# Quartered output matmuls for a state-space branch, its gated unit moved ahead of both halves of the other branch's projection, and one fixed order for the side matmuls

## The chip, the cores and the metric

The kernel runs on one core of a Trainium2 chip (trn2). The metric is device time in microseconds (us), the median of 3 runs. The engines are named as in the profile: PE (TensorE, matmuls), PEld (its weight loads), DVE (VectorE), ACT (ScalarE), POOL (GpSimd), SP (SyncE, which here only issues DMAs).

## The reference

One decoder block on 256 tokens of width 1024, all in float32. The normed input is projected by one matrix into seven parts, two branches are computed from them, merged through gates, projected, normed and added to the input; an MLP of hidden width 4096 follows.

```python
u = rms_norm(h, g_pre_mix)
z_ssm, z_q, z_k, z_v, z_ga, z_gb = split(u @ w_in)       # 512, 512, 512, 512, 1024, 1024
# branch A: S5, 32 groups x 16 channels, 64 complex states a group
x  = scan over time of (ab * x + bu)                      # ab, bu from lam, dt, b and z_ssm
y  = Re(C x) + d_skip * z_ssm
v  = gelu(y)
y_a = v * sigmoid(v @ w_glu + b_glu)                      # GLU
# branch B: causal attention, 8 heads x 64
y_b = softmax(q k^T / 8, causal) v
merged = sigmoid(z_ga) * (y_a @ w_branch_a) + sigmoid(z_gb) * (y_b @ w_branch_b)
h = h + rms_norm(merged @ w_out)
h = h + rms_norm(square(relu(rms_norm(h) @ w_ff1)) @ w_ff2)
```

## The kernel before

**Weights and main matmuls.** Every weight matrix is cut into pieces of 128 x 1024 floats (512 KB). SP loads a piece into one of 3 raw buffers (L154), ACT rounds it into a high part `w_hi` and DVE subtracts for a low part `w_lo` (both by `split`, L169 and L170), in 5 buffers; a raw buffer is free again when its `w_lo` is made. PE then does three matmuls for each product (high x high, high x low, low x high; `three`, L193 to L195). `chunk` runs this for 512 output columns with 256 tokens moving: 24 matmuls a piece. These are called the main matmuls here. The list `order` fixes the sequence of pieces: `ssm, k, q, v, ga0, ga1, gb0, gb1` (4 pieces each, numbers 0 to 31), then `bb0, glu, bb1, ba0, ba1` (2 each: branch B's projection in two halves, GLU, branch A's projection in two halves), then `wo` and the MLP.

**Side blocks.** The S5 state space and the attention are computed by small float32 matmuls between the main ones, each block inside `with soon()`. For S5 these are `transposes`, `states(0)`, `local`, `outputs(0)`, `states(1)`, `outputs(1)`; for the attention `scores`, `transposes`, `values` for two groups of heads, called by `att.group(0)` and `att.group(1)`. A float32 matmul runs as two instructions. `outputs(hf)` (L975) multiplies, for each of 8 pairs of groups, three full 128 x 128 weights by 64 moving columns: `Tl` with the input `U` (L982), `CA` with the two parts of the state `X` (L987), 24 matmuls a half. Its result has time steps and channels together on the partitions, four of one by 32 of the other; ACT applies gelu to it into `y` (L989).

**The shuffle.** GLU needs `v` with channels on the partitions and the steps along the row. `shuffle` makes it from `y` by 32 DMAs on SP's queue (L389), 16 for each half, each 32 partitions of 2 runs of 64 floats. `v` is then split into `v_h` and `v_l` and multiplied by the GLU weights; the result goes through sigmoid on ACT, a product on DVE and a split into `ya_h`, `ya_l`, which branch A's projection reads.

**What sets the order.** The code gives each instruction a priority (`at`), and a scheduler places instructions of each engine by priority and by when it takes their inputs to be ready; `follow` ties one instruction behind another on its engine. Each engine then runs its own list strictly in that order. `soon()` gives each side block a priority of its own, ahead of the main matmuls, so that the matmuls of several side blocks that are ready at one time are mixed one by one. PSUM has 4 `acc` and 4 `aux` buffers; side blocks and branch A's projection share `aux` in turn.

Of the kernel before, what the change touches and what calls it, by code (L numbers as in the profile page):

```python
# [9 lines left out]
F32 = mybir.dt.float32  # L10
# [8 lines left out]
P = 128  # L19
# [27 lines left out]
PARAMS, MATS_B, ROTATE, MATS_C, LOCAL, STATES, OUT, SHUFFLE = 30, 31, 32, 33, 33, (34, 36), (35, 37), (35, 37)  # L47
# [28 lines left out]
def tile_hybrid_block(ctx, tc, a, out):  # L76
# [13 lines left out]

    def soon():

        state["soon"] += 1
        return at(SOON + 0.001 * state["soon"])
# [40 lines left out]
    order += [(n, range(2)) for n in ("bb0", "glu", "bb1", "ba0", "ba1")]  # L135
# [8 lines left out]
    state = {"i": 0, "soon": 0}  # L144
# [47 lines left out]
    def three(o, wh, wl, xh, xl, start, stop):  # L192
        nc.tensor.matmul(o, lhsT=wh, rhs=xh, start=start, stop=False)  # L193
        nc.tensor.matmul(o, lhsT=wh, rhs=xl, start=False, stop=False)  # L194
        return nc.tensor.matmul(o, lhsT=wl, rhs=xh, start=False, stop=stop)  # L195
# [7 lines left out]
    def chunk(kts, xh, xl, get=acc):  # L203

        ps = [get(), get()]
        marks.clear()
        for kp in range(kts // 2):
            hi, lo = piece()
            for k2 in range(2):
                for m in range(4):  # L210
                    kt = 2 * kp + k2
                    ws = slice(512 * k2 + P * m, 512 * k2 + P * m + P)
                    marks[kt] = three(ps[m // 2][:, m % 2, :], hi[:, ws], lo[:, ws], xh[:, kt, :], xl[:, kt, :],
                          start=(kt == 0 and m % 2 == 0), stop=(kt == kts - 1 and m % 2 == 1))
        return ps
# [192 lines left out]
    shuffle(1)  # L408
    with at(ATT[1]):
        att.group(1)  # L410
# [45 lines left out]
    gate(1, 0)  # L456
    branch_b(0)
# [12 lines left out]
    gate(1, 1)  # L470
    branch_b(1)
# [200 lines left out]
class S5:  # L672


    def __init__(self, nc, sp, scratch, aux, ident, aidx, half_pi, dsk, spare, table, soon):
# [4 lines left out]
        self.bc = sp.tile([P, 4, NI, 16], F32, name="bc", tag="bcy")  # L680
# [220 lines left out]
    def transposes(self):  # L901

        nc, B4 = self.nc, self.B4
        self.y = self.sp.tile([P, NI, NB], F32, name="y", tag="bcy")
        self.B4T = B4T = [t.rearrange("p i b c -> p i (b c)") for t in B4]
        for i4 in range(4):
            for j in range(2):
                tp = self.aux((P, 4, P))
                with self.soon():
                    for i in range(4):  # L910
                        nc.tensor.transpose(tp[:, i, :], B4T[j][:, 4 * i4 + i, :], self.ident)
                nc.scalar.activation(B4T[j][:, 4 * i4:4 * i4 + 4, :], tp, AF.Copy)

    def local(self):
# [3 lines left out]
        with self.soon():  # L918
# [222 lines left out]
```

## Time and profile before

| | |
|---|---|
| median of 3 runs | 390.36 us (389.51 to 392.51) |
| the profiled execution | 389.2 us, of it the span 387.4 us |
| PE busy | 372.2 us, 96% of the span |
| DVE, ACT, POOL busy | 69%, 55%, 9% |
| chain that ended last | PE 88%, DMA 4%, DVE 2%, ACT 2%, issue 2% |

The busy time of PE says how much of the span had a matmul under way, not how fast they ran. Idle time of another engine costs nothing unless PE waits for it. So the rows to read are those where PE was idle or its matmuls were further apart than usual, and what came just before on the engine that released it.

### The profile page before, as it was taken

The numbers are of one execution on the slowest core, as the hardware profiler recorded it, in microseconds if no ns is written. First come the engines' busy times: TensorE is split into PE (matmuls) and PEld (weight loads), VectorE is DVE, ScalarE is ACT, GpSimd is POOL, SyncE is SP. The second block draws the span as 40 slices with busy tenths as digits, with TensorE's granted clock in tenths as the row PEclk, the third lists the DMA queues.
The fourth block names the chain that finished last, engine by engine and source line by source line (L and its number), as shares of the span: only waits on it lengthen the run. The fifth ranks groups of instructions, "written<-read, shape, count | busy, mean of one in ns | idle before, by whom it ended". The sixth has DMA issues, their size and how long they took to land.

```text
span 387.4 us, 6661 instructions
## 1 busy us (share of the span) xinstructions
PE 372.2 (96%) x2593; PEld 337.0 (87%) x2593; DVE 268.5 (69%) x459; ACT 213.3 (55%) x322; POOL 36.7 (9%) x46
## 2 busy tenths in 40 slices
PE   7999999999999996889999999999999999999993
PEld 6999989999897986788877989989898998989882
DVE  5899999988886264579595575665638375664734
ACT  4894559968773872645457563534444444443411
POOL 4006200001000000000010020100202020020200
PEclk9999999999999998999999999999999999999998
DMA  7956755544305056555643665665555555556302
GB/s 209 359 171 205 231 185 168 161 151 154 112 15 175 12 157 221 168 165 187 216 156 106 215 207 192 207 203 194 184 181 191 200 190 184 194 183 191 137 1 108
DMA packets 22160, 66.30 MB, mean 171 GB/s; under 512 B 5200, under 2 KB 5840, under 8 KB 22000
## 3 DMA queue, kind: packets, MB, share of 16 engines
q1 hardware_dynamic: 21184, 65.19, 51.9%
q0 software_dynamic: 512, 0.53, 0.6%
q8 instruction: 20, 0.33, 0.3%
q10 hardware_dynamic: 432, 0.17, 0.2%
q14 instruction: 12, 0.10, 0.1%
HBM read 63.77 MB, written 1.05 MB: 167 GB/s over the span
## 4 chain that ended last, share of the span: by engine, by line
PE 88%; DMA 4%; DVE 2%; ACT 2%; issue 2%; SPq 0%; DVEq 0%; POOLq 0%; POOL 0%; ACTq 0%
PE acc L200 11%; PE acc L198 11%; PE acc L199 11%; PE aux L194 8%; PE aux L195 8%; PE aux L193 8%; PE acc L193 7%; PE acc L195 7%; PE acc L194 7%; DMA w_raw<-in_w_in_dram 3%; PE aux L987 2%; PE aux L950 2%; PE aux L1013 1%; DMA v<-y 1%; PE aux L982 1%
## 5 line engine op out<-in xcount | busy, mean ns | idle before, releaser
L170 DVE TENSOR_TENSOR w_lo<-w_raw,w_hi 128x1024 fp32r<-128x1024 f32 (+2 forms) x119 | 139.6, 1178 | 79.3 <-ACT w_hi L169 78.7
L169 ACT ACTIVATE w_hi<-w_raw 128x1024 fp32r<-128x1024 f32 (+2 forms) x119 | 121.2, 1024 | 127.1 <-PE aux L194 38.2
L193 PE MATMUL acc<-xh,w_hi 128*128 128x256 f32 x224 | 63.4, 287 | 0.9 <-ACT w_hi L169 0.9
L194 PE MATMUL acc<-xl,w_hi 128*128 128x256 f32 x224 | 63.1, 286 | 0.0
L193 PE MATMUL aux<-h_h,w_hi 128*128 128x256 f32 x224 | 62.9, 281 | 0.0
L194 PE MATMUL aux<-h_l,w_hi 128*128 128x256 f32 x224 | 62.6, 280 | 0.0
L195 PE MATMUL aux<-h_h,w_lo 128*128 128x256 f32 x224 | 62.5, 280 | 0.0
L195 PE MATMUL acc<-xh,w_lo 128*128 128x256 f32 x224 | 60.2, 286 | 0.0
L198 PE MATMUL acc<-w_hi,f_h 128*128 128x512 f32 x128 | 50.2, 394 | 0.0
L199 PE MATMUL acc<-w_lo,f_h 128*128 128x512 f32 x128 | 50.1, 393 | 0.0
L200 PE MATMUL acc<-w_hi,f_l 128*128 128x512 f32 x128 | 49.6, 391 | 0.0
L193 PEld LDWEIGHTS acc<-xh,w_hi 128*128 128x128 f32 x224 | 43.0, 192 | 1.9 <-ACT w_hi L169 1.8
L194 PEld LDWEIGHTS acc<-xl,w_hi 128*128 128x128 f32 x224 | 43.1, 192 | 0.2 <-issue 0.2
L194 PEld LDWEIGHTS aux<-h_l,w_hi 128*128 128x128 f32 x224 | 42.1, 188 | 0.3
L193 PEld LDWEIGHTS aux<-h_h,w_hi 128*128 128x128 f32 x224 | 42.0, 188 | 0.3
L195 PEld LDWEIGHTS aux<-h_h,w_lo 128*128 128x128 f32 x224 | 42.0, 188 | 0.0
L195 PEld LDWEIGHTS acc<-xh,w_lo 128*128 128x128 f32 x224 | 41.2, 191 | 0.8 <-issue 0.4
L68 POOL TENSOR_TENSOR r<-r 128x512 f32<-128x512 f32 x14 | 17.8, 1288 | 131.6 <-ACT f_h L634 131.6
L200 PEld LDWEIGHTS acc<-w_hi,f_l 128*128 128x128 f32 x128 | 24.1, 188 | 5.5
L198 PEld LDWEIGHTS acc<-w_hi,f_h 128*128 128x128 f32 x128 | 24.1, 188 | 5.1
L199 PEld LDWEIGHTS acc<-w_lo,f_h 128*128 128x128 f32 x128 | 24.1, 188 | 4.8
L636 DVE TENSOR_TENSOR f_l<-r,f_h 128x512 fp32r<-128x512 f32 x14 | 15.3, 1097 | 6.5 <-POOL r L68 6.5
(245 smaller groups left out, 582.1 us busy)
## 6 DMA issues: line engine op xcount, KB each, us to landing
w_raw<-in_w_ff_dram SPq DMA_DIRECT2D x64, 512.0 KB, 4.8
w_raw<-in_w_in_dram SPq DMA_DIRECT2D x31, 512.0 KB, 4.1
w_raw<-in_w_out_dram SPq DMA_DIRECT2D x8, 512.0 KB, 4.6
w_raw<-in_w_bb_dram SPq DMA_DIRECT2D x4, 512.0 KB, 4.5
w_raw<-in_w_ba_dram SPq DMA_DIRECT2D x4, 512.0 KB, 5.6
w_raw<-in_w_glu_dram SPq DMA_DIRECT2D x2, 512.0 KB, 4.5
x_tok<-in_xt_dram SPq DMA_DIRECT2D x1, 1024.0 KB, 4.8
g_row<-in_rows_dram SPq DMA_DIRECT2D x2, 512.0 KB, 4.5
```

Of the source, the lines that this page charges most:

```text
L68: return nc.gpsimd.tensor_tensor(o, x, y, op=op)
L169: i = nc.scalar.activation(hi, src, AF.Copy)
L170: j = nc.vector.tensor_tensor(lo, src, hi.bitcast(F32), op=ALU.subtract)
L193: nc.tensor.matmul(o, lhsT=wh, rhs=xh, start=start, stop=False)
L194: nc.tensor.matmul(o, lhsT=wh, rhs=xl, start=False, stop=False)
L195: return nc.tensor.matmul(o, lhsT=wl, rhs=xh, start=False, stop=stop)
L198: first = nc.tensor.matmul(o, lhsT=xh, rhs=wh, start=start, stop=False)
L199: nc.tensor.matmul(o, lhsT=xh, rhs=wl, start=False, stop=False)
L200: nc.tensor.matmul(o, lhsT=xl, rhs=wh, start=False, stop=stop)
L636: nc.vector.tensor_sub(f_l[:, js, :], r, f_h[:, js, :].bitcast(F32))
L950: nc.tensor.matmul(S[j][:, i, :], lhsT=self.B4T[j][:, hf * H + i, :], rhs=U4[:, hf * H + i, :], start=(i == 0), stop=(i == H - 1))
L987: nc.tensor.matmul(py[:, i, :], lhsT=CA[j][:, ii, 1:5, :].rearrange("p d c -> p (d c)"), rhs=self.X[j][:, i, :], start=False, stop=(i == H ...
```

## The change

Four edits. (1) `outputs` is made in quarters: for each block of 2 rows of channels, each of the 4 steps and each of the 3 sources, four matmuls of 32 weight columns write the four 32-partition quarters of one PSUM tile, so that the result already has the layout of `v`; gelu writes `v` itself. That is 96 matmuls a half, in place of 24. (2) `shuffle`, its 32 DMAs and the tile `y` are gone. (3) GLU comes in front of both halves of branch B's projection, in the list of pieces and in the program. (4) Side blocks have one common priority and are tied to each other: within a block each matmul comes where it did, and a block's first matmul follows the last of the block before it; the first matmul of each `chunk` follows the last of the chunk before. The attention's `group` is cut into `weights` (scores, softmax's exponentials) and `outputs` (normalise, transpose, values), called around the S5 blocks.

```diff
     def soon():
-        state["soon"] += 1
-        return at(SOON + 0.001 * state["soon"])
+        first = []
+        def side(inst):
+            if not first and "side" in last_act:
+                follow(inst, last_act["side"])
+            first[:] = [inst]
+        with at(SOON):
+            yield side
+        last_act["side"] = first[0]
...
-    order += [(n, range(2)) for n in ("bb0", "glu", "bb1", "ba0", "ba1")]
+    order += [(n, range(2)) for n in ("glu", "bb0", "bb1", "ba0", "ba1")]
...
-    def shuffle(hf):
-        with at(SHUFFLE[hf]):
-            for b in range(4):
-                for q in range(4):
-                    nc.sync.dma_start(out=v[32 * q:32 * q + 32, 2 * hf:2 * hf + 2, b, :],
-                                      in_=s5.y[32 * b:32 * b + 32, 8 * hf + q:8 * hf + 8:4, :])
...
     with at(LOCAL):
         s5.local()
+    att.bind(qT, kT, v_tok)
+    with at(ATT[0]):
+        att.weights(0)
     with at(OUT[0]):
-        s5.outputs(0, att)
+        s5.outputs(0, v)
     with at(STATES[1]):
         s5.states(1)
-    att.bind(qT, kT, v_tok)
     with at(ATT[0]):
-        att.group(0)
+        att.outputs(0)
+    with at(ATT[1]):
+        att.weights(1)
     with at(OUT[1]):
-        s5.outputs(1, att)
-    shuffle(0)
-    shuffle(1)
+        s5.outputs(1, v)
     with at(ATT[1]):
-        att.group(1)
+        att.outputs(1)
...
-    gate(1, 0)
-    branch_b(0)
     ps = chunk(4, v_h, v_l)
...
-    gate(1, 1)
-    branch_b(1)
+    for c in range(2):
+        gate(1, c)
+        branch_b(c)
...
-    def outputs(self, hf, att):
+    def outputs(self, hf, v):
-        py = self.aux((P, H, NB))
-        with self.soon():
-            for i in range(H):
-                ii = hf * H + i
-                nc.tensor.matmul(py[:, i, :], lhsT=self.Tl[:, ii].rearrange("p b c -> p (b c)"), rhs=U4[:, ii, :],
-                                 start=(i == 0), stop=False)
-            for i in range(H):
-                ii = hf * H + i
-                for j in range(2):
-                    nc.tensor.matmul(py[:, i, :], lhsT=CA[j][:, ii, 1:5, :].rearrange("p d c -> p (d c)"),
-                                     rhs=self.X[j][:, i, :], start=False, stop=(i == H - 1 and j == 1))
-        self.table("gelu", nc.scalar.activation(self.y[:, hf * H:hf * H + H, :], py, AF.Gelu_apprx_tanh), "sin", "exp")
+        py = self.aux((P, 2, L, NB))
+        with self.soon() as side:
+            for m, b, src in ((m, b, src) for m in range(2) for b in range(L) for src in range(3)):
+                for q in range(4):
+                    i = 4 * m + q
+                    ii = hf * H + i
+                    w = self.Tl[:, ii, b, :] if src == 2 else CA[src][:, ii, 1 + b, :]
+                    side(nc.tensor.matmul(py[32 * q:32 * q + 32, m, b, :], lhsT=w,
+                                          rhs=U4[:, ii, :] if src == 2 else self.X[src][:, i, :],
+                                          start=(m == b == src == 0), stop=(m == 1 and b == L - 1 and src == 2)))
+        self.table("gelu", nc.scalar.activation(v[:, 2 * hf:2 * hf + 2], py, AF.Gelu_apprx_tanh), "sin", "exp")
```

Where instructions move, at three places. Rows are in the engine's order; a row gives line, operation and out<-in, with a count where the same row repeats.

PE, the second half of S5 and the attention. Before, rows from `values(0)` (L1062), `outputs(1)` (L982) and `scores(1)` (L1013) stand mixed:

```order
L1062 MATMUL aux<-pT_365,v_tok 64x256 x2
L982 MATMUL aux<-U_122,Tl 128x64
L1013 MATMUL aux<-kT,qT 128x128
L982 MATMUL aux<-U_122,Tl 128x64
L1013 MATMUL aux<-kT,qT 128x128
L1062 MATMUL aux<-pT_366,v_tok 64x128 x2
L1013 MATMUL aux<-kT,qT 128x128
L982 MATMUL aux<-U_122,Tl 128x64
```

After the change the same stretch has `scores(1)` (L1019), then the new `outputs(1)` (L992) by itself:

```order
L1019 MATMUL aux<-kT,qT 128x256 x2
L992 MATMUL aux<-Er,CA_126 32x64 x4
L992 MATMUL aux<-Ei,CA_127 32x64 x4
L992 MATMUL aux<-U_122,Tl 32x64 x4
L992 MATMUL aux<-Er,CA_126 32x64 x4
L992 MATMUL aux<-Ei,CA_127 32x64 x4
```

The mixing of blocks is gone, and each matmul of `outputs` fills 32 of the 128 output partitions. PE alternates between main matmuls and side blocks 7 times before, from `outputs(0)` on, and 10 times after, from `scores(0)` on.

SP, the DMA issues from the last `w_in` pieces on. Before:

```order
L154 DMA w_raw<-in_w_glu_dram 128x1024
L389 DMA v<-y 32x2x64
L154 DMA w_raw<-in_w_bb_dram 128x1024
L389 DMA v<-y 32x2x64 x10
L154 DMA w_raw<-in_w_bb_dram 128x1024
L389 DMA v<-y 32x2x64 x3
L154 DMA w_raw<-in_w_ba_dram 128x1024
L389 DMA v<-y 32x2x64 x3
```

After:

```order
L163 DMA w_raw<-in_w_in_dram 128x1024 x28
L163 DMA w_raw<-in_w_glu_dram 128x1024 x2
L163 DMA w_raw<-in_w_bb_dram 128x1024 x4
L451 DMA x_tok<-in_xt_dram 128x2048
L452 DMA g_row<-in_rows_dram 128x1024
L163 DMA w_raw<-in_w_ba_dram 128x1024 x4
```

The shuffle's DMAs no longer stand between the weight loads; `x_tok` and `g_row` (1.5 MB) now stand ahead of all four `ba` loads, before they stood ahead of the last two.

ACT, behind the second gelu. Before, `y` is made just ahead of these rows (L989); sigmoids (L423) and the attention's copies (L1046, L1051, L1065) follow, and `v_h` comes last:

```order
L423 ACT_TABLE_LOAD
L423 ACTIVATE sg_106<-sg_106 128x512 x2
L423 ACTIVATE sg_105<-sg_105 128x512 x4
L169 ACTIVATE w_hi<-w_raw 128x1024
L1046 ACTIVATE pT_365<-aux 128x512 x2
L1051 ACTIVATE pT_366<-aux 128x512
L169 ACTIVATE w_hi<-w_raw 128x1024 x2
L423 ACTIVATE sg_106<-sg_106 128x512
L1065 ACTIVATE yb_h<-aux 128x512
L423 ACTIVATE sg_106<-sg_106 128x512
L169 ACTIVATE w_hi<-w_raw 128x1024
L169 ACTIVATE v_h<-v 128x512 x2
```

After (exponentials L1033, gelu L995, sigmoids L431, copies L1052, L1057):

```order
L1033 ACTIVATE prob_364,sm_370<-prob_364,mx_368 128x256 x2
L178 ACTIVATE v_h<-v 128x512
L995 ACT_TABLE_LOAD
L995 ACTIVATE v<-aux 128x512
L431 ACT_TABLE_LOAD
L431 ACTIVATE sg_106<-sg_106 128x512 x2
L431 ACTIVATE sg_105<-sg_105 128x512 x4
L1052 ACTIVATE pT_365<-aux 128x512 x2
L178 ACTIVATE v_h<-v 128x512
```

The first half of `v_h` moved ahead of the second gelu, the second half now stands behind six sigmoids and the copies of `pT`.

## Rows read from the trace of the kernel before

**Rows 1.** The page: the chain that ended last, shares of the span by engine and by line.

```profile
PE 88%; DMA 4%; DVE 2%; ACT 2%; issue 2%; SPq 0%; DVEq 0%; POOLq 0%; POOL 0%; ACTq 0%
```

**Rows 2.** Windows view, the stretch behind the longest wait: its length, busy time of each engine (PE, PEld, DVE, ACT, POOL) with the count of instructions, PE's granted clock as a share of full speed, share of the DMA engines, GB/s.

```profile
149.25:163.20 13.95, 12.79 (x97) 12.60 (x97) 6.71 (x8) 6.57 (x11) 0.00 (x0) 0.88 0.66 228
```

**Rows 3.** The chain that ended last in order of time, 140 to 177 us: start, length, what.

```profile
143.28 4.88 DMA v<-y
...
152.91 0.21 PE acc L194
...
153.50 0.12 PE acc L194
```

**Rows 4.** Timeline of PE at its waits, and GLU's last matmul: start, length, instruction, and in brackets the idle time before and what ended it.

```profile
149.25 0.50 PE L193 MATMUL acc<-v_h,w_hi 128*128 128x256 f32 x2 [3.30 <-ACT v_h L169]
...
159.47 0.28 PE L195 MATMUL acc<-v_h,w_lo 128*128 128x256 f32 x1
...
163.17 0.74 PE L193 MATMUL aux<-ya_h,w_hi 128*128 128x256 f32 x4 [1.15 <-ACT ya_h L169]
165.67 0.39 PE L194 MATMUL aux<-ya_l,w_hi 128*128 128x256 f32 x1 [1.76 <-DVE ya_l L170]
```

**Rows 5.** Timeline of PE, 174 to 180 us: the first `w_out` matmul, behind the last of branch A's projection.

```profile
176.22 0.39 PE L198 MATMUL acc<-w_hi,mg_h 128*128 128x512 f32 x1
```

**Rows 6.** SP's queue: ten of the shuffle's issues (start, length), and the DMA view's line for them (KB each, median us from issue to landing).

```profile
122.01 14.76 SPq L389 DMA_DIRECT2D v<-y  x10
```

```profile
v<-y SPq DMA_DIRECT2D x32, 16.0 KB, 2.3
```

**Rows 7.** Timeline of PE, full-width side matmuls in a block: 16 instructions of `outputs(0)` up to the next instructions, which are the last two of `states(1)`, and the 32 of `states(0)`.

```profile
101.67 2.00 PE L987 MATMUL aux<-X,CA 128*128 128x64 f32 x16
103.50 0.39 PE L950 MATMUL aux<-U,B 128*128 128x64 f32 x2
```

```profile
77.94 3.68 PE L950 MATMUL aux<-U,B 128*128 128x64 f32 x32
```

**Rows 8.** Windows of 40 ns inside one block of `local` (L925: 16 instructions of 32 weight columns, 128 moving columns, four output quarters in turn): window, length, PE (instructions under way), PEld (loads under way).

```profile
86.10:86.14 0.04, 0.02 (x3) 0.02 (x4) 1.00 0.00 0
86.14:86.18 0.04, 0.04 (x4) 0.04 (x8) 1.00 0.00 0
...
86.46:86.50 0.04, 0.04 (x12) 0.04 (x4) 1.00 0.00 0
```

**Rows 9.** The same in windows of 20 ns for L929 (8 instructions of 32 weight columns on 32 partitions, 32 moving columns, four quarters in turn).

```profile
86.70:86.72 0.02, 0.02 (x4) 0.02 (x4) 1.00 0.00 0
...
86.74:86.76 0.02, 0.02 (x6) 0.02 (x8) 1.00 0.00 0
```

**Rows 10.** Line view of L925: duration in ns (min/median/max) of a weight load of 32 columns.

```profile
L925 PEld LDWEIGHTS aux<-CA,B x64: 105/109/111, 82.3 to 87.9; 128*32 128x32 f32 x64
```

**Rows 11.** Timeline of PE: the first and the last of the mixed stretch (16 instructions of L1062, 12 of L982 and 8 of L1013 start in it), and the same kinds in blocks.

```profile
117.65 0.65 PE L1062 MATMUL aux<-pT,v_tok 128*64 128x256 f32 x4
...
124.33 0.66 PE L982 MATMUL aux<-U,Tl 128*128 128x64 f32 x4
```

```profile
96.91 0.71 PE L1013 MATMUL aux<-kT,qT 64*128 64x128 f32 x4
97.55 0.43 PE L982 MATMUL aux<-U,Tl 128*128 128x64 f32 x2
```

```profile
137.70 0.65 PE L1062 MATMUL aux<-pT,v_tok 128*64 128x256 f32 x4
138.28 0.39 PE L195 MATMUL acc<-xh,w_lo 128*128 128x256 f32 x1
...
139.17 1.09 PE L1062 MATMUL aux<-pT,v_tok 128*64 128x128 f32 x12
140.19 0.38 PE L195 MATMUL acc<-yb_h,w_lo 128*128 128x256 f32 x1
```

**Rows 12.** Timeline of PE: 50 main matmuls start between the first and the last of these.

```profile
88.42 0.39 PE L193 MATMUL acc<-xh,w_hi 128*128 128x256 f32 x1
88.65 0.28 PE L194 MATMUL acc<-xl,w_hi 128*128 128x256 f32 x1
...
94.42 0.33 PE L982 MATMUL aux<-U,Tl 128*128 128x64 f32 x2
```

**Rows 13.** Timeline of ACT: the second gelu, a table load, six sigmoids, two copies of `pT`.

```profile
130.44 0.60 ACT L989 ACTIVATE y<-aux 128x512 f32<-128x512 f32 x1
131.06 1.28 ACT L423 ACT_TABLE_LOAD   x1
132.35 3.24 ACT L423 ACTIVATE sg<-sg 128x512 f32<-128x512 f32 x6
...
136.45 1.06 ACT L1046 ACTIVATE pT<-aux 128x512 f32<-128x512 f32 x2
```

**Rows 14.** Timeline of DVE: a normalisation of the softmax, a `w_lo`, the last state of `states(1)`, and one of the masked maxima of `scores`.

```profile
113.25 1.13 DVE L1034 TENSOR_SCALAR prob<-prob,sm 128x256 f32<-128x256 f32 x4
114.30 1.22 DVE L170 TENSOR_TENSOR w_lo<-w_raw,w_hi 128x1024 fp32r<-128x1024 f32 x1
...
116.03 0.68 DVE L699 TENSOR_TENSOR Ei<-wpzA,wpzB 128x504 f32<-128x504 f32 x1
...
126.53 0.42 DVE L1020 CUSTOM_DVE_ANT_0 prob<-aux,shp 128x256 f32<-128x256 f32 x1 [0.77 <-PE aux L1013]
```

More of the change, by code (lines that the diff above doesn't have):

```diff
@@ L192, in three @@
     def three(o, wh, wl, xh, xl, start, stop):
[L193 removed]
+        first = nc.tensor.matmul(o, lhsT=wh, rhs=xh, start=start, stop=False)
         nc.tensor.matmul(o, lhsT=wh, rhs=xl, start=False, stop=False)
[L195 removed]
+        return first, nc.tensor.matmul(o, lhsT=wl, rhs=xh, start=False, stop=stop)
     def three_tok(o, xh, xl, wh, wl, start, stop):
@@ L212, in chunk @@
                     ws = slice(512 * k2 + P * m, 512 * k2 + P * m + P)
-                    marks[kt] = three(ps[m // 2][:, m % 2, :], hi[:, ws], lo[:, ws], xh[:, kt, :], xl[:, kt, :],
+                    first, marks[kt] = three(ps[m // 2][:, m % 2, :], hi[:, ws], lo[:, ws], xh[:, kt, :], xl[:, kt, :],
                           start=(kt == 0 and m % 2 == 0), stop=(kt == kts - 1 and m % 2 == 1))
+                    if earlier is not None:
+                        follow(first, earlier)
+                        earlier = None
         return ps
@@ L917, in local @@
         pt = self.aux((P, 4, P))
-        with self.soon():
+        with self.soon() as side:
             for ct in range(4):
@@ L946, in states @@
         S = [aux((P, H, NB)), aux((P, H, NB))]
-        with self.soon():
+        with self.soon() as side:
             for j in range(2):
                 for i in range(H):
-                    nc.tensor.matmul(S[j][:, i, :], lhsT=self.B4T[j][:, hf * H + i, :], rhs=U4[:, hf * H + i, :],
-                                     start=(i == 0), stop=(i == H - 1))
+                    side(nc.tensor.matmul(S[j][:, i, :], lhsT=self.B4T[j][:, hf * H + i, :], rhs=U4[:, hf * H + i, :],
+                                          start=(i == 0), stop=(i == H - 1)))
         er, ei, R = self.E[hf]
@@ L1008, in scores @@
         sc = [self.aux((P, 2, n)), self.aux((P, 2, n))]
-        with self.soon():
+        with self.soon() as side:
             for e in range(2):
@@ L1012, in scores @@
                     rows = slice(64 * par, 64 * par + 64)
-                    nc.tensor.matmul(sc[par][:, e, :], lhsT=self.qT[rows, 2 * g + e, qt * P:qt * P + P],
-                                     rhs=self.kT[rows, 2 * g + e, 0:n], start=(e == 0), stop=(e == 1))
+                    side(nc.tensor.matmul(sc[par][:, e, :], lhsT=self.qT[rows, 2 * g + e, qt * P:qt * P + P],
+                                          rhs=self.kT[rows, 2 * g + e, 0:n], start=(e == 0), stop=(e == 1)))
         return sc
@@ L1055, in values @@
         yp = self.aux((P, 2, T))
-        with self.soon():
+        with self.soon() as side:
             for e in range(2):
@@ L1061, in values @@
                         hc = slice(64 * (4 * g + h), 64 * (4 * g + h) + 64)
-                        nc.tensor.matmul(yp[64 * par:64 * par + 64, e, qs], lhsT=v_tok[:, kt, hc], rhs=pT[:, h, :],
-                                         start=(e == 0 and kt == 0), stop=(e == 1 and kt == 1))
+                        side(nc.tensor.matmul(yp[64 * par:64 * par + 64, e, qs], lhsT=v_tok[:, kt, hc], rhs=pT[:, h, :],
+                                              start=(e == 0 and kt == 0), stop=(e == 1 and kt == 1)))
         gs = slice(2 * g, 2 * g + 2)
@@ L1074, in group, with outputs @@
             self.exp(qt)
+    def outputs(self, g):
         for qt in range(2):
```

35 lines of the change are left out of this document (18 added, 17 removed).

## The prediction

> **What bounds the kernel now.** I read the shares of the chain that ended last first: PE holds 88% of it, DMA 4% [rows 1]. So the kernel is a PE kernel, and time is won where PE has less to do or waits less. The same chain in order of time shows the one long piece that is not PE: the shuffle's last DMA from 143.28 us, 4.88 us long [rows 3]. PE's timeline then gives the waits themselves. Before GLU's first matmul PE stood idle for 3.30 us, released by `v_h`. Before branch A's projection it stood idle for 1.15 and 1.76 us, released by `ya_h` and `ya_l` [rows 4]: GLU's last matmuls are just ahead there, and its sigmoid, product and split are exposed. [...] The chain's matmuls stand 0.21 us apart up to 152.91 us, and 0.12 from 153.50 on [rows 3]. Everything before the first side blocks and behind the first `w_out` matmul at 176.22 us [rows 5] runs the same instructions before and after.
>
> **Removed: the shuffle (3.3 + 1.7 us).** gelu writes `v`, so the 32 DMAs go, and with them the wait for the last of them. A shuffle DMA took 2.3 us from issue to landing, and ten of them held SP's queue for 14.76 us, weight loads behind them [rows 6]. All 3.30 us of idle time and the 1.7 us of slow clock go if no other wait of that length takes their place; that is the third rival.
>
> **Moved: GLU in front (2.9 us).** GLU's chain of sigmoid, product and split now has 96 matmuls of branch B's projection behind it, some 11 us of PE by 0.118 us a matmul (49 in 94.42 - 88.65 us [rows 12]). Before, the chain ran from GLU's last matmul at 159.47 us to the last release at 165.67, 6.2 us [rows 4]. That fits under 11, so 1.15 + 1.76 = 2.9 us go. The loads of `x_tok` and `g_row` are now ahead of all `ba` loads on SP; they are 1.5 MB, about 6.6 us at the 228 GB/s of [rows 2], and the first `ba` piece is needed 17 us of matmuls (GLU and both `bb` halves) after the last main chunk. This costs nothing.
>
> **Made anew: `outputs` (3.8 us won, from 0 to 5.8).** Before, 16 full-width instructions took 1.83 us, 0.114 each [rows 7], so the 48 of a half 5.5 us. After, a half has 96 matmuls, 192 instructions, in 48 groups of four quarters. Two rows bound a group. `local` does the same with 128 moving columns: the four instructions start together, and the four groups of a block start between 86.12 and 86.47 us, 0.115 us a group [rows 8]. L929 does it with 32 moving columns: one group starts by 86.70, the next by 86.755, 0.055 us [rows 9]. Here 64 columns move, and the straight line between gives 0.055 + 0.060 x 32 / 96 = 0.075 us, 3.6 us a half. I take that; the ends are 2.6 and 5.5 us. Two halves win 2 x (5.5 - 3.6) = 3.8 us.
>
> [...]
>
> **Untied: mixed side blocks (2.1 us).** From 117.65 to 124.33 us, 6.68 us, 16 instructions of L1062, 12 of L982 and 8 of L1013 ran mixed one by one. In blocks, 16 of L1062 took 0.58 + 1.02 = 1.60 us, and four of L1013 0.64 [rows 11]; 12 of L982 at 0.114 are 1.37. Together 4.25 us, so mixing cost 2.4 us. The new order has no mixing, but alternates with main matmuls three times more; the first main matmul behind a block took 0.23 us instead of 0.118 [rows 12], so 0.3 us is given back.
>
> **Added: waits of PE behind tied blocks (2.7 us lost).** All side blocks now wait for the one before, and PE runs its list in order, so a late block holds the main matmuls behind it, too. I walked PE's new list from 88.42 us, where `local` ends. `scores(0)` 2.4 us, 74 main matmuls 8.7, `outputs(0)` 3.6, `states(1)` 3.7 (as the 32 instructions of `states(0)` [rows 7]): 106.8 us. Then 12 transposes at 0.114, 72 main matmuls, `values(0)` 1.6, `scores(1)` 2.4 and `outputs(1)` 3.6 bring PE to the second group's transposes at about 124.2 us. They need the softmax normalised on DVE. Before, the last state of `states(1)` was made by 116.71 us, 13.0 us behind its last matmul at about 103.7 [rows 7, 14]. With the same chain it is made at 119.8 us now. Behind it stand `yb_l` (0.7, as the last state's 504 columns), eight maxima (four at 0.42 and four of half the width, 2.4), two `w_lo` (1.2 each) and two normalisations (1.13 and about 0.8 at half the width) [rows 14], 7.4 us: 127.2 us. Transposes of the first head can begin a little earlier, so PE loses about 2 us. At GLU I find no wait longer than 0.4 us: gelu, its table, sigmoids' table, six sigmoids and two copies are 7.5 us of ACT [rows 13] in front of `values(1)`, and PE has 48 main matmuls, 5.6 us, behind those transposes to cover them; `v_h` and gelu's table can run while DVE normalises. The first group's transposes find gelu(0) some 0.3 us late. Together 2.7 us.
>
> **The sum.** 3.3 + 1.7 + 2.9 + 3.8 + 2.1 - 2.7 = 11.1 us. The profiled execution took 389.2 us; the median of the runs is 390.36, 1.2 above it. So 378.1 us against that execution, and 379.3 as a median.
>
> **Rivals.** First: ACT and DVE set the pace from `states(1)` to GLU. For it speaks that DVE's chain is 13.0 us long and that the walk already ends in a wait for it; against it, all long waits of PE before lay behind this stretch [rows 4]. Then a faster `outputs` and the unmixing win nothing, the added waits are their own size: 3.3 + 1.7 + 2.9 = 7.9 us, 382.5 us.
>
> Second: weight loads of a quarter don't run beside the matmuls of other quarters. Then a group costs a load of 0.109 us [rows 10] and half of 0.115 for the matmul, 0.166 us, 8.0 a half. PE gets later by 8.8 us, which covers the 2.7 us of added waits: 11.1 - 8.8 + 2.7 = 5.0, 385.4 us. Against it, eight loads were under way beside four matmuls from 86.14 to 86.18 us [rows 8]. [...]
>
> Third: the wait moves instead of going. `v_h`'s second half now stands behind gelu, six sigmoids and the copies of `pT`; if that chain is 3 us late, PE idles in front of GLU as before and the clock falls again: 11.1 - 5.0 = 6.1, 384.3 us.
>
> Fourth, the other side: the quarters run one after another at a full-width instruction's 0.114 us. Then a half takes 192 x 0.114 = 21.9 us, 32.8 more for two. The other terms win 10.0 us, and PE is too late for the added waits: 390.36 + 32.8 - 10.0 = 413 us. It decides from 5.5 + 5.0 = 10.5 us a half on, 0.22 us a group, twice what [rows 8] show.
>
> **How the numbers follow.** The forecast gets 0.56, the first rival 0.22, the third 0.08, the second 0.06, the fourth 0.04; 0.04 is left for a group at its lower bound with no added wait, 374.6 us. The forecast's own range is 377 to 381.5. I predict 379.3 us, and 376.5 to 384.5 holds the forecast, the first rival and part of the third. One per cent of 390.36, about what a measurement of this kernel can tell from no change, ends at 386.5 and 394.3: faster 0.92, within it 0.04 (part of the second), slower 0.04.
>
> **What would show it.** `outputs`' 192 instructions in 3.6 us, 2.6 to 5.5; PE's idle time in front of GLU under 0.5 us and granted clock 1.0 from 130 to 165 us; no idle time in front of branch A's projection; the first `w_out` matmul near 165 us instead of 176.22; a wait of PE for DVE of some 2 us at the second transposes. I am wrong if a group of four takes more than 0.115 us, if PE idles in front of `values(1)` or GLU, or if gaps appear behind 176 us, where I assumed nothing changes.

## The result, and the profile after

The changed kernel takes 379.65 us (median of 4, 379.20 to 380.60), the kernel before 389.94 beside it: ratio 0.9728, 95% interval 0.9678 to 0.9778. In a second group of runs the same kernel took 378.68 us against 390.44 (ratio 0.9681, 0.9634 to 0.9727). The forecast was 379.3. The profiled execution has a span of 378.2 us, 9.2 less than before. Medians are of all runs, while the ratios leave out the few runs that the chip ran at a lower granted clock and some per cent longer.

The chain that ended last, shares by engine (before: [rows 1]):

```profile
PE 89%; DMA 3%; ACT 3%; issue 2%; DVE 1%; DVEq 0%; POOLq 0%; POOL 0%; ACTq 0%
```

The shuffle's piece of DMA is gone from the chain, ACT has one point more. PE's timeline where it had waited in [rows 4], and the first `w_out` matmul ([rows 5]): no brackets, so no idle time, in front of GLU or of branch A's projection.

```profile
138.01 0.28 PE L202 MATMUL acc<-v_h,w_hi 128*128 128x256 f32 x1
...
156.41 0.28 PE L202 MATMUL aux<-ya_h,w_hi 128*128 128x256 f32 x1
...
167.29 0.39 PE L207 MATMUL acc<-w_hi,mg_h 128*128 128x512 f32 x1
```

`outputs(1)` in the timeline: rows of 8 instructions stand 0.11 us apart, so four quarters take 0.056 us, and 24 such rows reach from 127.11 us to the first transposes at 129.93, where PE then waits for the normalised softmax.

```profile
127.11 0.32 PE L992 MATMUL aux<-Er,CA 128*32 128x64 f32 x8
127.25 0.29 PE L992 MATMUL aux<-Ei,CA 128*32 128x64 f32 x8
127.36 0.29 PE L992 MATMUL aux<-U,Tl 128*32 128x64 f32 x8
...
129.93 0.33 PE L1050 MATMUL aux<-shp,prob 128*128 128x128 f32 x1
130.97 0.33 PE L1051 MATMUL aux<-shp,prob 128*128 128x128 f32 x1 [0.71 <-DVE prob L1040]
```

Two things are new. Inside `outputs(0)` PE stands still for 1.22 us with nothing that it waits for, and soon after it everything runs slowly: the 32 instructions of `states(1)` take 5.47 us (3.68 in [rows 7]).

```profile
103.91 0.39 PE L992 MATMUL aux<-X,CA 128*32 128x64 f32 x10
105.51 0.26 PE L992 MATMUL aux<-X,CA 128*32 128x64 f32 x3 [1.22 <-issue]
...
105.86 5.47 PE L956 MATMUL aux<-U,B 128*128 128x64 f32 x32
```

Windows view, columns as in [rows 2]. The granted clock is 0.69 over 11.15 us, and 0.50 in the middle of it, from 110 to 112 us: an estimated 0.31 x 11.15 = 3.5 us. Where it was 0.88 before, it is 1.00.

```profile
106.50:117.65 11.15, 11.15 (x70) 10.64 (x69) 10.82 (x18) 5.33 (x10) 0.00 (x0) 0.69 0.39 129
110.00:112.00 2.00, 2.00 (x12) 2.00 (x12) 1.71 (x4) 0.06 (x1) 0.00 (x0) 0.50 0.65 225
149.25:163.20 13.95, 13.95 (x125) 13.95 (x124) 11.60 (x16) 6.56 (x8) 0.00 (x0) 1.00 0.62 195
```

### The profile page after: what moved, and what is told of

Read it like the earlier page. It is cut to its first block, busy times and chain, and to the rows that moved or that the text cites. A ratio compares the mean times of both kernels' runs of the same rounds, so it can differ in the third digit from the quotient of the medians.

```text
span 378.2 us, 7188 instructions
## 1 busy us (share of the span) xinstructions
PE 365.8 (97%) x2881; PEld 332.1 (88%) x2881; DVE 267.9 (71%) x459; ACT 213.0 (56%) x322; POOL 36.6 (10%) x46
## 4 chain that ended last, share of the span: by engine, by line
PE 89%; DMA 3%; ACT 3%; issue 2%; DVE 1%; DVEq 0%; POOLq 0%; POOL 0%; ACTq 0%
PE acc L209 11%; PE acc L207 11%; PE acc L208 11%; PE aux L204 8%; PE aux L202 8%; PE aux L203 8%; PE acc L204 8%; PE acc L202 7%; PE acc L203 7%; DMA w_raw<-in_w_in_dram 3%; PE aux L956 2%; PE aux L1019 1%; PE aux L917 1%; PE aux L992 1%; PE aux L1068 1%
## 5 line engine op out<-in xcount | busy, mean ns | idle before, releaser
L203 PE MATMUL aux<-h_l,w_hi 128*128 128x256 f32 x224 | 62.5, 279 | 0.0
L204 PE MATMUL acc<-xh,w_lo 128*128 128x256 f32 x224 | 61.0, 288 | 0.0
```

Of the source, the lines that this page charges most:

```text
L204: return first, nc.tensor.matmul(o, lhsT=wl, rhs=xh, start=False, stop=stop)
```

## The experiments

The base is the changed kernel of the second group, `after_again`, 378.7 us. The kernel before took 390.4 us beside `after_again`, `full_width`, `untied` and `states_first`, 389.6 beside `glu_between`, `with_shuffle`, `late_turns` and `cut_and_late`, and 390.0 beside the other four; between kernels of different groups the ratios are the fairer comparison. Besides the time, the table gives for each profile the stretch from the first S5 transpose to the first `w_out` matmul, which holds all that the change touches; the first transpose itself comes between 69.3 and 72.4 us, in instructions that are the same in all kernels. The stretch is split by PE's timeline: the time from each row's start to the next row's, less the idle time in brackets, added up by kind (main matmuls; `outputs`; the other side blocks; idle).

| kernel | median us | ratio to before (95%) | stretch | main | outputs | other | idle |
|---|---|---|---|---|---|---|---|
| before | 390.4 | | 106.3 | 62.5 | 11.7 | 25.9 | 6.2 |
| the change, first profile | 379.65 | 0.9728 (0.9678 to 0.9778) | 96.0 | 61.0 | 6.1 | 27.0 | 1.9 |
| `after_again` | 378.68 | 0.9681 (0.9634 to 0.9727) | 94.2 | 60.2 | 6.1 | 24.8 | 3.2 |
| `ties_alone` | 379.66 | 0.9745 (0.9698 to 0.9792) | 96.3 | 61.1 | 10.5 | 24.0 | 0.7 |
| `untied` | 385.62 | 0.9860 (0.9814 to 0.9905) | 101.5 | 60.7 | 10.4 | 29.5 | 0.9 |
| `with_shuffle` | 386.95 | 0.9945 (0.9918 to 0.9971) | 104.9 | 63.8 | 10.5 | 24.0 | 6.6 |
| `full_width` | 379.67 | 0.9716 (0.9666 to 0.9766) | 95.2 | 60.5 | 10.5 | 24.0 | 0.3 |
| `glu_between` | 379.50 | 0.9753 (0.9717 to 0.9790) | 97.5 | 62.3 | 6.1 | 27.0 | 2.2 |
| `states_first` | 379.28 | 0.9704 (0.9656 to 0.9753) | 95.5 | 61.6 | 6.1 | 24.6 | 3.3 |
| `quarters_apart` | 387.69 | 0.9945 (0.9916 to 0.9974) | 103.9 | 60.3 | 19.1 | 24.3 | 0.2 |
| `outputs_twice` | 393.92 | 1.0103 (1.0067 to 1.0139) | 109.3 | 60.4 | 14.4 | 24.9 | 9.4 |
| `late_turns` | 376.98 | 0.9676 (0.9652 to 0.9700) | 93.4 | 60.3 | 6.1 | 24.6 | 2.5 |
| `cut_and_late` | 378.10 | 0.9715 (0.9679 to 0.9751) | 94.6 | 60.6 | 5.9 | 24.6 | 3.6 |
| `late_free` | 377.10 | 0.9679 (0.9625 to 0.9732) | 91.7 | 60.0 | 6.1 | 24.5 | 1.2 |

At a granted clock of 1.00 the main matmuls ran at two paces, 0.118 and 0.113 us each. In the last part of the stretch it was 0.113 in most of these profiles, but 0.118 in `untied`, `with_shuffle`, `glu_between` and `states_first`. Over the 240 matmuls of GLU and both projections that is 1.1 us, so a difference of this size in the column "main" says nothing about the edit; what sets the pace is open.

**`after_again`**: no edit.

> The changed kernel once more, as the base of this group and for a second profile. Forecast's theory: about 379.6 us. Two things of the first profile are to be seen again or not: PE idle for 1.22 us inside the first block of outputs with nothing that it waits for, and the granted clock at 0.69 in the 11 us behind it. If the idle time starts the slow clock, each profile with the one has the other. If the small matmuls alone do it, the clock falls in every profile, also without the idle time. PE's late start of the first profile (side blocks 1.3 us later than before, in rows that are the same) should not come back if it is scatter between executions.

Waits of PE, by what they waited for (us in total, times, longest):

```profile
PE aux L1051 <- DVE prob L1040: 1.9, 1, 1.9
...
PE aux L992 <- issue: 0.9, 1, 0.9
...
PE aux L1050 <- ACT v L995: 0.3, 1, 0.3
```

The idle time came again, the slow clock did not: 1.00 in all windows from 0 to 180 us. Neither of the two simple rules holds. PE is 3.5 us earlier by the clock, and 1.5 of it goes into the waits behind (1.92 + 0.32 in place of 0.71): the stretch is only 1.8 us shorter. The first S5 transpose came at 70.5 us, between the kernel before (70.0) and the first profile (71.3).

**`ties_alone`**: the fourth edit by itself, that is the ties and the new order of the blocks.

Against the kernel before:

```diff
     def soon():
-        state["soon"] += 1
-        return at(SOON + 0.001 * state["soon"])
+        first = []
+        def side(inst):
+            if not first and "side" in last_act:
+                follow(inst, last_act["side"])
...
+                    if earlier is not None:
+                        follow(first, earlier)
...
-        att.group(0)
+        att.weights(0)
...
+        att.outputs(0)
```

> The kernel before with the ties of side blocks and the blocks' new order alone: full-width outputs, y, the shuffle and GLU between the bb halves as before. Theory of the sum: unmixing wins 2.1 us less the added waits; PE comes to the shuffle's end no later than before, and the shuffle starts when outputs(1) is done, some 4 us earlier than before, so the wait in front of GLU shrinks as well: 2 to 5 us faster than before, 385 to 388. Rival (what is won in front of the shuffle is lost waiting for it): the wait in front of GLU grows from 3.3 us by what the unmixing won, no change, 390.

379.66 us: the fourth edit alone brings all of the gain that can be measured. The timeline of ACT (second gelu and `v_h`) and PE:

```profile
126.70 0.60 ACT L1007 ACTIVATE y<-aux 128x512 f32<-128x512 f32 x1 [0.75 <-PE aux L1005]
142.39 1.15 ACT L178 ACTIVATE v_h<-v 128x512 fp32r<-128x512 f32 x2 [1.50 <-DMA v<-y]
```

```profile
143.07 0.50 PE L202 MATMUL acc<-v_h,w_hi 128*128 128x256 f32 x2 [0.39 <-ACT v_h L178]
...
149.19 0.28 PE L202 MATMUL acc<-yb_h,w_hi 128*128 128x256 f32 x1
...
154.63 0.39 PE L202 MATMUL aux<-ya_h,w_hi 128*128 128x256 f32 x2
```

`v_h` in the kernel before:

```profile
148.57 1.15 ACT L169 ACTIVATE v_h<-v 128x512 fp32r<-128x512 f32 x2 [4.62 <-DMA v<-y]
```

All 32 shuffle DMAs are there. But PE's wait ends 6.2 us earlier (143.07 instead of 149.25), while PE itself comes only 3.3 earlier (142.68 instead of 145.95), so the wait falls from 3.30 to 0.39 us (and 0.28 for `v_l`). Of the 6.2 us, 3.7 are the second gelu, at 126.70 instead of 130.44 us [rows 13]; the other 2.4 are a shorter way from gelu to `v_h`. SP's timeline shows the last shuffle DMA of the kernel before behind one more weight load, the third since that gelu:

```profile
142.70 0.53 SPq L154 DMA_DIRECT2D w_raw<-in_w_ba_dram  x1
143.28 0.58 SPq L389 DMA_DIRECT2D v<-y  x1
```

In `ties_alone` the last four stand behind the second load:

```profile
136.66 0.45 SPq L163 DMA_DIRECT2D w_raw<-in_w_ba_dram  x1
137.16 2.50 SPq L402 DMA_DIRECT2D v<-y  x4
```

The whole second `bb` half now lies between GLU and `ya_h`, and no wait is left there. In the kernel before, its own timeline shows that it did not lie there:

```profile
149.59 0.28 PE L193 MATMUL acc<-yb_h,w_hi 128*128 128x256 f32 x1
...
154.37 0.28 PE L194 MATMUL acc<-v_l,w_hi 128*128 128x256 f32 x1
...
159.59 0.28 PE L195 MATMUL acc<-yb_h,w_lo 128*128 128x256 f32 x1
```

Behind GLU's first two matmuls the scheduler had put 28 of the second `bb` half, then GLU's other 46, and only 20 behind GLU. Those 20 (2.4 us) were all that covered GLU's chain of 6.2 us [rows 4].

**`untied`**: the change without the ties of the side blocks; the ties of `chunk` and the new order of the blocks stay.

```diff
-        with at(SOON):
-            yield side
-        last_act["side"] = first[0]
+        state["soon"] += 1
+        with at(SOON + 0.001 * state["soon"]):
+            yield lambda inst: inst
```

> The changed kernel with the old priorities in place of the ties between side blocks; quarters, no shuffle and GLU in front are kept. Theory of the sum: mixing costs 2.1 us again, the wait of 0.7 us at the second transposes goes: 1.4 us slower, about 381. Rival (ACT and DVE set the pace): within 0.5 us of the change, the mixed stretch only takes up time in which PE would wait. A mixed block spreads its instructions, so if the 1.22 us of idle time come from a dense run of small instructions, it shrinks.

7 us slower than the change, five times the expected 1.4. Mixed, the quarters lose their speed:

```profile
101.91 0.43 PE L949 MATMUL aux<-U,B 128*128 128x64 f32 x2
102.27 0.30 PE L985 MATMUL aux<-X,CA 128*32 128x64 f32 x2
102.50 0.43 PE L949 MATMUL aux<-U,B 128*128 128x64 f32 x2
102.86 0.30 PE L985 MATMUL aux<-X,CA 128*32 128x64 f32 x2
```

One quarter matmul of 2 instructions takes 0.23 us when its neighbours are full-width matmuls, which take 0.36 in place of 0.23. `outputs` needs 10.4 us of PE, as much as in full width, and the other blocks 4.7 more than in `after_again`.

**`quarters_apart`**: the same quarters, neighbours in one quarter.

```diff
-            for m, b, src in ((m, b, src) for m in range(2) for b in range(L) for src in range(3)):
-                for q in range(4):
+            for m, q in ((m, q) for m in range(2) for q in range(4)):
+                for b, src in ((b, src) for b in range(L) for src in range(3)):
```

> The changed kernel with the same 192 quarter matmuls of outputs in another order: all 12 matmuls of one quarter, then those of the next, so that neighbours write the same quarter of the output partitions. Theory that the speed comes from four neighbours in four quarters that run at the same time: each instruction now takes as long as a full-width one, 0.114 us, 21.9 us a half in place of 2.8: 38 us more, less the wait at the second transposes, about 415. Rival (a quarter is fast by itself, because it has 32 columns of weights): 0.03 us an instruction or less, within 5 us of the change. A block that runs at the slow pace should show no idle time without a releaser inside it, if that comes from instructions that are fetched too late.

Between the two. The timeline shows a matmul (2 instructions) every 0.11 us:

```profile
103.00 0.28 PE L992 MATMUL aux<-U,Tl 128*32 128x64 f32 x2
103.11 0.39 PE L992 MATMUL aux<-X,CA 128*32 128x64 f32 x4
103.33 0.28 PE L992 MATMUL aux<-U,Tl 128*32 128x64 f32 x2
```

With the steps from quarter to quarter it is 19.1 / 384 = 0.050 us an instruction, 0.014 with four different quarters side by side. So four abreast are worth a factor of 3.5, and a quarter by itself is still twice as fast as a full-width instruction (0.114 us [rows 7]). There is no idle time without a releaser in this profile.

**`full_width`**: quarters undone, the shuffle left out.

```diff
-                    side(nc.tensor.matmul(py[32 * q:32 * q + 32, m, b, :], lhsT=w,
...
+                side(nc.tensor.matmul(py[:, i, :], lhsT=self.Tl[:, ii].rearrange("p b c -> p (b c)"), rhs=U4[:, ii, :],
...
+                    side(nc.tensor.matmul(py[:, i, :], lhsT=CA[j][:, ii, 1:5, :].rearrange("p d c -> p (d c)"),
...
+        self.table("gelu", nc.scalar.activation(v[:, 2 * hf:2 * hf + 2].rearrange("p m b a -> p (m b) a"), py,
```

> The changed kernel with outputs as before the change, 24 full-width matmuls a half instead of 96 quarters; there is still no shuffle, gelu writes v without the change of layout, so v holds the right numbers in the wrong places and the output is not the reference's. It leaves the quarters out and keeps the rest. Theory of the sum (PE sets the time in this stretch): PE needs 2 x (5.5 - 2.8) = 5.4 us more, and the idle 1.2 us is gone since there are a quarter of the instructions. If the idle time started the slow clock, its 3.5 us are won back too: 5.4 - 1.2 - 3.5 = 0.7 us slower than the change. If the clock falls for another reason: 4.2 us slower. Rival (ACT and DVE set the pace up to the second transposes): no slower than the change by more than 0.5 us whatever the clock does, because PE's lost time was covered by their chain.

1.0 us slower than the base in the median and in the stretch; the intervals of the two ratios overlap. PE needs 4.4 us more for `outputs`, but 2.9 us of idle time are gone (3.2 to 0.3): the time that quarters save comes back as waits for ACT and DVE and as the idle time of their own block. The rival holds for most of it. The granted clock is 1.00 up to 180 us. Against `ties_alone`, which has the shuffle and GLU's old place and is otherwise the same, the median is equal and the stretch 1.1 us shorter: once the ties are there, leaving out the shuffle and moving GLU are together worth some 1 us, no more than the noise.

**`with_shuffle`**: the full-width `outputs`, `y` and `shuffle` of the kernel before put into the changed kernel, GLU in front.

```diff
+                side(nc.tensor.matmul(py[:, i, :], lhsT=self.Tl[:, ii].rearrange("p b c -> p (b c)"), rhs=U4[:, ii, :],
...
+        self.table("gelu", nc.scalar.activation(self.y[:, hf * H:hf * H + H, :], py,
...
         s5.outputs(1, v)
+    shuffle(0)
+    shuffle(1)
```

> The changed kernel with the full-width outputs, y and the 32 shuffle DMAs put back; ties, the order of blocks and GLU in front are kept. With the full-width outputs but no shuffle the kernel took 379.7 us. Theory of the sum: GLU now has no bb half in front of it, so the shuffle's end meets PE 48 matmuls (5.6 us) earlier than before the change: the 3.3 us of idle time become 8 to 9, the slow clock behind it costs 1.7 or more, together some 10 us above full_width, 389 to 391, which is no gain at all over the kernel before. Rival (the ties alone are worth most of the gain): the tied order brings outputs and so the shuffle earlier by 4 to 5 us, the idle time stays at 3 to 4 us, and the time is about 384.

```profile
144.73 0.79 PE L202 MATMUL acc<-v_h,w_hi 128*128 128x256 f32 x2 [6.57 <-ACT v_h L178]
```

```profile
144.73:158.68 13.95, 13.95 (x100) 13.66 (x101) 7.94 (x11) 7.35 (x13) 0.00 (x0) 0.84 0.55 188
```

7.3 us slower than `full_width` (8.9 by the ratios), its stretch 9.7 longer. The idle time is 6.57 us and the granted clock behind it 0.84 (second fence, windows view): 6.6 + 0.16 x 13.95 = 8.8 of the 9.7 us; the slower pace of the main matmuls is about the rest. `ties_alone` differs from this kernel by GLU's place alone: with the shuffle, GLU in front costs over 7 us. Both theories were half right: GLU has lost the 5.6 us of a `bb` half in front of it, but the second gelu came 2.6 us earlier than before (127.84 us).

**`glu_between`**: GLU back between the `bb` halves, in the list and in the program.

```diff
-    order += [(n, range(2)) for n in ("glu", "bb0", "bb1", "ba0", "ba1")]
+    order += [(n, range(2)) for n in ("bb0", "glu", "bb1", "ba0", "ba1")]
...
+    gate(1, 0)
+    branch_b(0)
     ps = chunk(4, v_h, v_l)
```

> The changed kernel with GLU between the two bb halves again, in the list of pieces and in the program; no shuffle, quarters and ties are kept. Theory of the sum: 1.15 + 1.76 = 2.9 us of waits in front of branch A's projection come back, since only one bb half (48 matmuls, 5.6 us) stands behind GLU to cover its chain of 6.2 us and what ACT and DVE put ahead of it: 2.9 us slower than the change, about 381.5. Rival (the chain is covered by one half as well, because ACT is free of the second gelu and the shuffle's late v_h): under 1 us slower. Against the base of about 378.7 in the group before.

No wait in front of `ya_h`: one whole half covers the chain, as the rival says. Whether the time bears it out is open: the median is 0.8 us above the base, but by the ratios (0.9753 and 0.9681, intervals that just overlap) it is 2.8 us. Against the first profile of the change, whose clock fell in the same windows, the stretch is 1.5 us longer, 0.34 of it a wait for `yb_l` and about 1.1 the slower pace of the main matmuls.

**`states_first`**: `states(1)` ahead of `outputs(0)`.

```diff
+    with at(STATES[1]):
+        s5.states(1)
     with at(OUT[0]):
         s5.outputs(0, v)
-    with at(STATES[1]):
-        s5.states(1)
```

> The changed kernel with states(1) ahead of outputs(0) in the tied order; the same instructions. DVE's chain behind states(1) starts some 9 us earlier (32 matmuls right behind scores(0)), so the second group's softmax should be ready when PE comes to it. Theory of the sum: the wait of 0.7 us at the second transposes goes and nothing else, 0.7 us faster, 379.0. Rival (ACT and DVE set the pace from states(1) to the second transposes): what PE lost to the slow clock had been covered; with the chain earlier nothing is covered, and the 0.7 us are won only if no new wait stands at the first transposes or at gelu, where ACT is. If idle time inside outputs(0) comes from the dense run of instructions, it stays, since the block is as dense as before.

No change that can be measured. PE came to the second transposes earlier too (17 main matmuls between the two parts of `scores(1)`, 41 before), so most of the wait there stayed, 1.55 us, and 0.40 us came in front of the first transposes. The idle time inside `outputs(0)` was 1.33 us, with the clock at 1.00.

**`late_turns`, `cut_and_late`, `late_free`**: what the waits are worth.

```diff
+    follow(att.turn, marks[5])
...
+        s5.outputs(0, v, (0,))
     with at(STATES[1]):
         s5.states(1)
+    with at(OUT[0]):
+        s5.outputs(0, v, (1,))
...
             sigmoid(s, s)
+            follow(last_act["sigmoid"], att.turned)
```

The first line, in all three, ties the first of the second transposes (`turn`) behind a main matmul; the four lines on `outputs` are in `cut_and_late` alone, the last in `late_free` alone (`turned` is the last copy of `pT`).

> The changed kernel with one more tie: the second group's transposes follow the 72nd of the 96 matmuls of the last w_in chunk, 24 main matmuls (2.8 us) later than in the change. Nothing else differs. Theory that PE's wait for the normalised softmax is lost time: the wait of 1.9 us (0.7 in the first profile) goes, the values still lie inside GLU's and bb's main matmuls, and the time falls by 0.7 to 1.9 us, to about 377.3. Rival (the wait only moves on, because the copies of pT on ACT and the values come later too and yb is late for bb): a new wait in front of values(1) or of bb of the same length, time as the base, 378.7.

> late_turns, and the first block of outputs cut in two with states(1) between its halves, so that no run of quarters is longer than 80 instructions there; the second block stays whole. If the idle time of 0.9 to 1.3 us with nothing to wait for comes from a dense run of some 170 small instructions, it is gone in the first block and a wait of this kind may now show at the second block instead (there it was inside the wait for DVE, if at all). Then 1 us faster than late_turns, about 376.3. If the idle time has to do with the place in the program and not with the density, it stays, and the time is that of late_turns.

> late_turns, and the gates' sigmoids tied behind the last copy of pT on ACT. In late_turns PE waited 1.33 us in front of values(1) for the copies of pT, which stood on ACT behind a table load, six sigmoids, v_h and a w_hi. Theory that this wait is lost time: it goes and the time falls by about 1.3 us, from 377.0 to 375.7, if the sigmoids, now later, are done before bb needs yb_h, which stands behind them. Rival (a stretch with no slack left on ACT: the wait goes to yb_h in front of bb or to GLU's sigmoids): time as late_turns.

`late_turns` took 376.98 us (376.61 to 377.46), 1.7 less than the base, but the kernel before was 0.8 faster in its group as well, and the ratios (0.9676 and 0.9681) show no gain. In its profile the wait for DVE is gone, a new one of 1.33 us stands in front of `values(1)`, and the stretch is 0.8 us shorter. ACT's timeline shows why: six sigmoids stood ahead of the copies of `pT`.

```profile
131.23 3.24 ACT L432 ACTIVATE sg<-sg 128x512 f32<-128x512 f32 x6
134.37 0.62 ACT L178 ACTIVATE v_h<-v 128x512 fp32r<-128x512 f32 x1
134.89 1.04 ACT L178 ACTIVATE w_hi<-w_raw 128x1024 fp32r<-128x1024 f32 x1
135.84 1.06 ACT L1056 ACTIVATE pT<-aux 128x512 f32<-128x512 f32 x2
```

In `cut_and_late` (378.10 us, 376.3 expected) the idle time inside `outputs(0)`, whose longest run is now 96 instructions, is gone, and the whole second block, 192 in a row, shows none either; but the first transposes now wait 1.24 us for DVE, which has still to read what `states(1)` made, and the copies of `pT` come 2.13 us late. In `late_free` nothing is left but the 1.16 us inside `outputs(0)`, and the stretch is the shortest, 91.7 us. Its runs fall in two groups: 375.45, 375.70 and 375.82 us at a mean granted clock of 0.997 to 0.998, and 378.37, 378.89 and 379.30 at 0.982 to 0.983. So three runs took what was expected (375.7), and the other three some 3 us more at the lower clock. The ratio (0.9679) is again that of the base: what these waits are worth is seen in the stretch, not in the medians.

**`outputs_twice`**: each group of four issued twice.

```diff
-            for m, b, src in ((m, b, src) for m in range(2) for b in range(L) for src in range(3)):
+            for m, b, src, again in ((m, b, src, again) for m in range(2) for b in range(L) for src in range(3) for again in range(2)):
```

> The changed kernel with every group of four quarters issued twice in a row, so v is made of doubled sums (192 matmuls a half, 384 instructions); the output is not the reference's. Theory of the sum with the measured pace: 2 x 2.7 = 5.4 us more, less the 0.7 to 1.9 us of the wait at the second transposes, which the later PE covers: about 382.5. If PE runs out of instructions in a dense run (the idle time of 0.9 to 1.3 us with nothing to wait for, after 170 instructions of the first block), a run twice as long has such idle time at least twice in the first block and also in the second: 3 to 5 us more on top, 385 to 387. If the idle time belongs to one place in the program, there is one of 1.1 us, as before.

15 us slower than the base, far more than either theory: 8.3 us more of `outputs`, and four idle times with nothing to wait for, in both blocks, 9.4 us together (timeline):

```profile
104.02 0.36 PE L992 MATMUL aux<-U,Tl 128*32 128x64 f32 x11 [1.02 <-issue]
...
109.67 0.54 PE L992 MATMUL aux<-X,CA 128*32 128x64 f32 x11 [3.66 <-issue]
...
134.69 0.25 PE L992 MATMUL aux<-Er,CA 128*32 128x64 f32 x3 [1.36 <-issue]
...
140.06 0.29 PE L992 MATMUL aux<-U,Tl 128*32 128x64 f32 x3 [3.38 <-issue]
```

## Why the prediction was right, and where it was not

**The time was right, the terms nearly so.** In `after_again`, whose clock stays up, the six can be read: 3.3 us in front of GLU, 1.7 us of slow clock and 2.9 us in front of `ya_h` are gone in full; `outputs` in blocks fell from 10.5 to 6.1 us, 4.4 for 3.8; the mixing cost (11.7 - 10.5) + (25.9 - 24.8) = 2.3 for 2.1, with the 10.5 of `ties_alone`; idle time added is 3.2 for 2.7, of which 0.9 is the idle time inside `outputs(0)` that the term did not hold. The 1.7 us are an estimate, 0.12 x 13.95 us by the granted clock of 0.88 in [rows 2]. All six make 11.4, and the stretch is 12.0 us shorter; the other 0.6 lie in the main matmuls. Of what was to be seen, `outputs` in 3.6 us a half took 3.0, the wait at the second transposes was 0.71 and 1.92 us for "some 2", and the first `w_out` matmul came at 167.29 and 164.70 for 165. That the first median came within 0.4 us of the forecast is in part luck: its profile holds 3.5 us of slow clock that no term had, and the profiled execution took 380.0 us where 378.1 was forecast.

**What the terms were put down to was wrong: each to one edit, where another would end the same wait.** The step "Removed: the shuffle (3.3 + 1.7 us)" gave the wait to the 32 DMAs, and "Moved: GLU in front (2.9 us)" gave the other waits to GLU's place. `ties_alone` has the shuffle and the old place and loses nearly all of both waits. The first fell because `v_h` came 6.2 us earlier and PE only 3.3; the second because the engine's order has 48 matmuls behind GLU, as the ties of `chunk` demand, where 20 had been. The 14.76 us for which ten shuffle DMAs held SP's queue [rows 6] were mostly a wait, too: after the first of them at 122.01 us, the other nine start at 131.07, behind the second gelu. [rows 4] showed that GLU's last matmuls stood just ahead of `ya_h`; I took that for the effect of the list of pieces, and did not read which `bb` matmuls stood between 149.59 and 159.59 us. "Untied: mixed side blocks (2.1 us)" was thus the term that fell shortest: the fourth edit is worth 10 us by itself, in part through waits that I had counted under the other edits. How much each of its two kinds of ties brings, and how much the new order of the blocks, was not tried apart.

**The edits don't add up, in both directions.** The change without the ties of side blocks takes 385.6 us, the fourth edit without the other three 379.7, all four 378.7 to 379.7. GLU in front needs the shuffle gone (`with_shuffle`, 387.0), and the quarters need the ties (`untied`): I had taken their pace from `local`, which stood in one block [rows 8], and did not ask what mixing would do to it.

**The first rival** (ACT and DVE set the pace) had the larger part of `outputs`: of 4.4 us saved on PE, `full_width` against the base shows 1.0 in the time, hardly clear of the noise. That the total came out is because the added waits stood in the sum. The profile of `late_free`, where two of them are gone by order alone and no new one has come, shows that these waits were not a matter of ACT or DVE being full.

**The second and the fourth rival** fell: four quarters take 0.056 us with their loads, and even neighbours in one quarter need 0.050 us an instruction, 9.5 us a half, below the 10.5 from which the fourth decided. In the change 8 loads of 0.11 us each (median 110 ns in the line view) start in every 0.11 us, and from 102.30 to 102.34 us 10 loads and 17 matmuls were under way (windows view).

**The third** did not come. Idle time and a slow clock stood elsewhere, 1.2 us in front of `states(1)` and 3.5 us behind it, which no step had; that the one brought the other is not shown, since `after_again` has the idle time without the slow clock.

## What to carry to other kernels

When a change holds several edits, ask of every wait which of them would end it alone: two edits that each remove the same wait win it once. Ahead of a wait, read in the engine's order what really stands between producer and consumer; the list in the program said 48 matmuls, the order 20. And where a saving rests on neighbours (four quarters side by side), the edit that keeps them neighbours is part of its price.

## What the runs showed of the hardware

**PE stood idle in dense runs of small instructions.** In six profiles of whole blocks of quarters PE stood still inside `outputs(0)` for 0.94 to 1.33 us, after some 170 of its instructions at 0.014 us each, with nothing to wait for; not in `cut_and_late` (cut block), `untied` (mixed) or `quarters_apart` (0.050 us each), and four times in `outputs_twice`. In these runs it takes the density, but that is not enough: `outputs(1)`, 192 instructions at the same pace, has no such idle time inside it in any of the six. The DMA view shows a packet of the instruction queue under way in the first profile at 102.80 us, 1.5 us before PE stopped:

```profile
q8 instruction: 1, 0.02, 78.8%
```

It ended at 104.06 us, and PE went on 1.45 us later. Read in the same way, all ten idle times, from 0.94 to 3.66 us long, ended 1.33 to 1.55 us after the end of a packet of this queue; the two longest (3.66 and 3.38 us) have the whole packet inside them. In `outputs_twice` the second idle time of either block came after another 128 matmuls and 128 loads (windows view, second block, from inside the one idle time to inside the other):

```profile
134.00:140.00 6.00, 1.99 (x128) 1.84 (x128) 1.39 (x6) 0.00 (x0) 0.00 (x0) 1.00 0.36 109
```

So the end of the idle time follows the instruction packet in every case, which speaks for PE waiting for instructions. That it did is my estimate from these times; no run changed the arrival of instructions by itself.

**The clock after a short idle time is not settled.** Behind 1.22 and 1.11 us of it the granted clock fell (the change, 0.69 over 11.15 us, and `glu_between`, 0.76 from 104 to 118 us), behind 0.94, 1.14, 1.16 and 1.33 it did not, nor behind waits of 1.92 us (`after_again`) and 2.13 us (`cut_and_late`): the mean granted clock of these profiled executions is 0.994 to 0.998, and 0.981 and 0.983 in the two where it fell. Of the six runs of `late_free` three had a lower clock, 0.982 to 0.983. Behind the idle times of over 3 us in these stretches it was low each time: 0.88 behind 3.30 us in the kernel before [rows 2], 0.84 behind 6.57 us in `with_shuffle`, and in `outputs_twice` 0.85 from 109.70 to 120 us and 0.66 from 140 to 145 us, behind 3.66 and 3.38 us. What decides after a short one stays open.
